# Splitting the ScalarE and VectorE parts of single steps into stages of their own in a Conformer/Mamba-2 trunk layer

## The chip, the cores and the metric

The kernel runs on one core of a Trainium2 chip. The metric is the device time of one execution in microseconds, the median of several runs. The core has a matrix engine (TensorE, PE in the profile), three engines for element-wise work (VectorE or DVE, ScalarE or ACT, GpSimd or POOL), and an engine that only issues transfers here (SyncE, SP). Each engine runs its own instructions strictly in the order in which the program issued them, and waits at an instruction until its operands are ready. The program writes these orders out by hand.

## The reference

One layer for two request groups (1024 prompt rows and 32 rows of a decoding group) with shared weights. All branch inputs come out of one wide projection:

```python
proj = x @ w_in + b_in
a_val, a_glu, a_gate, z, xbc, dt_raw, g_a, g_b, g_p = jnp.split(proj, idx, axis=-1)
u = a_val * jax.nn.sigmoid(a_glu)
u, new_buf_a = causal_dwconv(u, buf_a, conv_a_w, conv_a_b)            # width 31
u = jax.nn.silu(layer_norm(u, norm_a_g, norm_a_b)) * jax.nn.silu(a_gate)
out_a = u @ w_a_out
xbc, new_buf_b = causal_dwconv(xbc, buf_b, conv_b_w, conv_b_b)        # width 4
xs, Bm, Cm = jnp.split(jax.nn.silu(xbc), [...], axis=-1)
dt = jax.nn.softplus(dt_raw + dt_bias);  A = -jnp.exp(a_log)
y, h_new = ssd_scan(xs_h, dt, A, Bm, Cm, h0)                          # in chunks
y = y + d_skip * xs_h
out_b = gated_rmsnorm(y, z, gnorm_w) @ w_b_out                        # y * silu(z), rms over 4 groups
merged = sigmoid(g_a) * out_a + sigmoid(g_b) * out_b
ple = sigmoid(g_p) * (p @ w_ple)
x_new = layer_norm(alpha * x + merged @ w_out + ple, ln_g, ln_b)
```

The model width is 1024, the inner width of the Mamba-2 branch 2048 in 4 groups of 8 heads of 64, and the state has 128 columns. The outputs are the two groups' rows and the new caches and states. All is float32.

## The kernel before, in words

Tiles hold 128 channels in the partitions and the 1056 rows (NT) along the free dimension. A float32 product is made of three reduced-precision products: every operand is split into a high part (`act`, L198, on ScalarE) and a low part, the difference (`tt`, L184, on VectorE).

The program is a sequence of numbered slots. After a start (the per-layer embedding, the products for dt, the first splits) come 30 pair slots. Each computes two tiles of 128 channels of the wide projection with seven products j = 0 to 6 instead of eight (a Strassen scheme, with sums T3, T4 and so on of halves of x, and combined weights w_0 to w_6, whose high and low parts carry an h or l: w_5l is the low part for product 5). A product takes 24 matmuls. From `S_CL` = 31 on come 28 classic slots, each one tile of the projection in 72 matmuls. In most of the slots 31 to 67 an SSD chunk runs beside it: `load_l`, `decay`, then in the next slot `prep`, `pe_o`, `carry` and `pe_d`, and `update` at the start of the slot after that. From `S_OB` = 59 on come the slots of the output projection of the B branch, from `S_OA` = 71 those of the A branch, from `S_Q3` = 79 the last quarter of B, and `S_WO` = 83 begins the last product with w_out and the final LayerNorm.

What else is to be done is put beside these products by `at(slot, stage, fn)`. A slot runs its stages in a fixed order, and that order is the order on every engine. In a pair slot `ld0`, `ld`, `st`, `d0`, `a0` and `d1` come after the evacuation of product 0, `a1` after product 2, `pm` and `a2` after product 4, `d2` after product 5, `pe` and `end` at the close; the split of the next weights stands after every product. In a classic slot it is `ld0`, the weights' load, `ld`, `st`, `d0`, the weights' split, `a0`, `d1`, then the products' three column groups with `a1` after the first and `pm` and `a2` after the second, then `d2`, `pe`, `end`. The evacuations of TensorE's results are ScalarE instructions between the stages, so whatever stands ahead of them on ScalarE delays them.

The queue `fill` holds the taps of the A branch's convolution of width 31, 31 items a channel tile. `run_fill(limit)` issues them until the planner's sum of VectorE's modelled time in this slot, `dve[0]`, passes the limit: 2820 ns a product in a pair slot (less 300), 11000 in a classic slot, 14200 if the slot has a chunk. `ca_flush` in slot 34 issues what is left. Tiles of working memory come from pools; `tget` takes the one that has been free the longest, and waits (by its release) for a store that still reads it.

SP's queue carries the loads, and the stores as long as the slot is below 31; later stores go through GpSimd's queue. The combined weights come by accumulating transfers on GpSimd's queue in the pair phase.

The names that matter: `dt0` to `dt10` make dt and its decays (a softplus by series, a scan, two reciprocals, repacking), `DT9` is the slot of its transposes. `t_split` and `x_sum` make the operands of the products. `cw_load` and `cw_sum` read w_out for its column means. `z_tile` handles a tile of z with `gate`, `square`, `add`, `spill`. `ln_center`, `ln_square`, `ca_away` and `ln_var` make the channel LayerNorm's centred tiles and variance, with `A0` = 37. `y_load`, `y_hi` and `y_lo` bring back, scale and split the gated SSD result. `base_tiles` adds embedding and residual; `wo_load` and `wo_split` bring four tiles of w_out early.

Of the kernel before, what the change touches and what calls it, by code (L numbers as in the profile page):

```python
# [61 lines left out]
def pair_tiles():  # L62
# [6 lines left out]
    return [G(0), G(2), C(0), G(8), G(4), G(10), C(1), G(6), G(12), C(2), Z(14), G(14), C(3), Z(12), G(16), C(4), G(18),  # L69
# [67 lines left out]
def emit(nc, tc, I, O, ctx):  # L137
# [114 lines left out]
    busy = set()  # L252
# [54 lines left out]
    def slot(s, nm, nk, rhs, evac):  # L307
# [312 lines left out]
    def dt1():  # L620
# [5 lines left out]
        act(small[:H, 41:42], col(C_DT + 2, 1, H), AF.Sigmoid)
        act(small[:H, 42:43], col(C_DT + 2, 1, H), AF.Sigmoid, scale=-1.0)
        nc.vector.reciprocal(small[:H, 42:43], small[:H, 42:43])
        tt(small[:H, 41:42], small[:H, 41:42], small[:H, 42:43], ALU.mult)
# [22 lines left out]
    def dt3():
# [12 lines left out]
    def dt4():  # L665

        v, t, e = dtt["v"], dtt["t"], dtt["cum"]
# [4 lines left out]
    def dt5():
# [297 lines left out]
    def ssd_group(g, s0, XS, Bt_, Ct_):  # L970
# [15 lines left out]
        for i in range(9):  # L986
# [150 lines left out]
    def z_tile(g, j, zt, s):  # L1137
# [724 lines left out]
```

## Time and profile before

| | us |
|---|---|
| median of 3 runs | 1599.21 |
| lowest and highest | 1598.11, 1600.18 |
| the profiled execution | 1598.68 |
| its span | 1597.0 |
| TensorE busy | 1515.9 (95%) |
| VectorE busy | 1207.4 (76%) |
| ScalarE busy | 863.7 (54%) |
| mean granted TensorE clock | 0.979 |

The span is the time from the first to the last recorded instruction. Busy times overlap between engines. A granted clock of 1 is full speed; the profile gives it for every stretch, and a stretch in which TensorE had half its clock shows as a mean below 1. The row of a wait names the waiting engine's instruction and the instruction or transfer that released it, with the total, the count and the longest in us. Slot 1 begins at 44.41, slot 7 at 191.49, slot 30 at 664.69, slot 59 at 1144.37 and slot 79 at 1431.98.

### The profile page before, as it was taken

The page shows a single profiled execution, that of the slowest core. Times are in us where ns is not written, and L with a number is a line of the kernel's source. Part 1 is how long each engine was busy: PE and PEld are TensorE (multiplying, and loading weights), DVE is VectorE, ACT ScalarE, POOL GpSimd, SP SyncE. Part 2 cuts the span into 40 slices and gives each one's busy share as a digit, 9 for nine tenths or more (in the row PEclk, how much of TensorE's full clock was granted, in tenths as well). Part 3 has the DMA queues.
Part 4 walks back from the last instruction along what each step waited for, and adds up shares of the span by engine and source line. Part 5 has one row for each costly group of instructions (what it writes and reads, how often), then busy time and mean ns, then how long its engine had stood idle before and what let it go on. Part 6 is the DMA issues. An engine that isn't in the chain of part 4 may idle for free.

```text
span 1597.0 us, 27638 instructions
## 1 busy us (share of the span) xinstructions
PE 1515.9 (95%) x10967; PEld 1462.7 (92%) x10967; DVE 1207.4 (76%) x1647; ACT 863.7 (54%) x1491; POOL 288.1 (18%) x443
## 2 busy tenths in 40 slices
PE   7889999999999999998999889999998999999897
PEld 7889999999999999997999879889987989998897
DVE  6657898998988898789883768476856787577654
ACT  6536444444434443554774767678776366443333
POOL 1223343343333333211110110010000000000000
PEclk9989999999999999999999989999999999999998
DMA  9867978888676788447884574645473556545122
GB/s 313 239 173 177 268 199 228 238 205 210 161 180 167 180 220 206 108 134 240 268 261 146 159 181 110 182 116 140 163 234 93 158 178 234 199 177 183 31 90 74
DMA packets 156418, 288.43 MB, mean 181 GB/s; under 512 B 27120, under 2 KB 83456, under 8 KB 156288
## 3 DMA queue, kind: packets, MB, share of 16 engines
q1 hardware_dynamic: 112224, 176.60, 35.2%
q0 software_dynamic: 44064, 110.07, 27.7%
q8 instruction: 86, 1.41, 0.4%
q14 instruction: 44, 0.36, 0.1%
HBM read 226.14 MB, written 60.46 MB: 179 GB/s over the span
## 4 chain that ended last, share of the span: by engine, by line
PE 71%; DVE 10%; ACT 7%; DMA 6%; issue 5%; SPq 0%; POOL 0%; ACTq 0%; DVEq 0%; POOLq 0%
PE ps L211 70%; DVE acc_t L184 1%; ACT L_t L198 1%; DMA zt_u<-d_z 1%; DMA cat_u<-d_ca 1%; DVE cao_u L188 1%; DMA d_gate<-ga_t 1%; DMA yraw_t<-d_yn 1%; DMA zt_z<-d_z 1%; ACT whi L198 1%; PE ps L1017 1%; ACT L198 1%; DMA wq<-in_wp 1%; DVE cae_u L188 1%; SPq L201 0%
## 5 line engine op out<-in xcount | busy, mean ns | idle before, releaser
L493 POOL DMA_DIRECT2D s<-in_w x150 | 131.8, 907 | 260.3 <-DMA s<-in_w 204.4
L188 DVE SCALAR_TENSOR_TENSOR cae_u<-uin_u,par,cae_u 128x1086 f32<-128x1086 f32 x120 | 161.2, 1344 | 0.0
L188 DVE SCALAR_TENSOR_TENSOR cao_u<-uin_u,par,cao_u 128x1086 f32<-128x1086 f32 x112 | 150.5, 1344 | 0.0
L184 DVE TENSOR_TENSOR wlo<-wraw,whi 128x1024 fp32r<-128x1024 f32 x53 | 64.9, 1224 | 78.8 <-ACT whi L198 78.6
L198 ACT ACT_TABLE_LOAD x74 | 94.9, 1283 | 3.0 <-DMA zt_t<-d_z 0.9
L211 PE MATMUL ps<-t3l,w_4h 128*128 128x264 f32 x240 | 69.7, 291 | 6.9 <-ACT ga_t L198 6.9
L211 PE MATMUL ps<-n2l,w_2h 128*128 128x264 f32 x240 | 69.3, 289 | 7.0 <-ACT ga_t L198 7.0
L198 ACT ACTIVATE whi<-wraw 128x1024 fp32r<-128x1024 f32 x53 | 56.0, 1056 | 35.3 <-PE ps L211 26.2
L198 ACT ACTIVATE gb_t<-ps,par 128x528 f32<-128x528 f32 x32 | 22.5, 702 | 94.5 <-PE ps L211 90.5
L488 POOL DMA_DIRECT2D s<-in_w x84 | 46.3, 552 | 132.7 <-issue 40.0
L211 PE MATMUL ps<-t3h,w_4l 128*128 128x264 f32 x240 | 69.8, 291 | 0.0
L211 PE MATMUL ps<-t3h,w_4h 128*128 128x264 f32 x240 | 69.4, 289 | 0.0
L211 PE MATMUL ps<-n2h,w_2h 128*128 128x264 f32 x240 | 69.3, 289 | 0.0
L488 POOL DMA_DIRECT2D r<-in_w x85 | 61.1, 761 | 43.3 <-DVE w_0l L184 15.1
L211 PE MATMUL ps<-n2h,w_2l 128*128 128x264 f32 x240 | 68.9, 287 | 0.0
L211 PE MATMUL ps<-t4h,w_6h 128*128 128x264 f32 x240 | 68.4, 285 | 0.0
L211 PE MATMUL ps<-t4l,w_6h 128*128 128x264 f32 x240 | 68.1, 284 | 0.0
L211 PE MATMUL ps<-t4h,w_6l 128*128 128x264 f32 x240 | 67.9, 283 | 0.0
L198 ACT ACTIVATE ga_t<-ps,par 128x528 f32<-128x528 f32 x36 | 25.2, 700 | 57.4 <-PE ps L211 57.4
L211 PEld LDWEIGHTS ps<-t3l,w_4h 128*128 128x128 f32 x240 | 46.2, 192 | 7.2 <-ACT ga_t L198 7.2
L211 PEld LDWEIGHTS ps<-n2l,w_2h 128*128 128x128 f32 x240 | 46.1, 192 | 7.2 <-ACT ga_t L198 7.2
L198 ACT ACTIVATE ps<-ps 128x528 f32<-128x528 f32 x28 | 16.7, 595 | 64.2 <-PE ps L211 64.2
(1120 smaller groups left out, 6075.8 us busy)
## 6 DMA issues: line engine op xcount, KB each, us to landing
s<-in_w POOLq DMA_DIRECT2D x234, 256.0 KB, 4.7
r<-in_w POOLq DMA_DIRECT2D x85, 256.0 KB, 5.4
wraw<-in_w SPq DMA_DIRECT2D x27, 512.0 KB, 8.6
wraw<-in_wb SPq DMA_DIRECT2D x16, 512.0 KB, 3.9
E<-d_expa SPq DMA_DIRECT2D x56, 128.0 KB, 8.7
d_gate<-ga_t SPq DMA_DIRECT2D x12, 528.0 KB, 6.1
yraw_t<-d_yn SPq DMA_DIRECT2D x12, 528.0 KB, 6.4
L_z<-d_accp SPq DMA_DIRECT2D x12, 512.0 KB, 9.0
```

The costliest lines, as they stand in the source:

```text
L184: nc.vector.tensor_tensor(out, a, b, op)
L188: nc.vector.scalar_tensor_tensor(out, a, s, b, op0, op1)
L198: nc.scalar.activation(out, a, f, **kw)
L211: nc.tensor.matmul(out, l, r, start=start, stop=stop, skip_group_check=more)
L488: (nc.gpsimd if cur[0] else nc.sync).dma_start(t, pw_src(i, PARTS[n][0]))
L493: nc.gpsimd.dma_start(pr[i, n], pw_src(i, (PARTS[n] + ("12",))[k]), accum_op=ALU.add)
L1017: nc.tensor.transpose(pX[:nt, j * P:(j + 1) * P], XS[j][:, sl], ident)
```

## The change

Steps that had their ScalarE and VectorE parts in one stage get a stage for each. No matmul is added or removed. In detail:

- The T3 splits, T4 sums and T4 splits are issued in stages a0, d1 and a1 of slot 1, no longer ahead of it.
- The dt chain is cut into 18 steps instead of 13, spread over slots 2 to 9. `pk` goes; the repacked values live in `e`, and the reciprocal of 528 columns becomes two of 264.
- The loads and sums of w_out for the means (`cw_load`, `cw_sum`) go from slots 1 and 2 to slots 2, 3, 4, 7 and 8.
- The order of the gate pairs in the pair slots changes.
- `run_fill`'s limit in a classic slot counts 1100 for a chunk's slot and 2400 for the slot after it, on 11000.
- `z_tile`: gate from pm to d2, square from a2 to the next slot's a0, add from d1 to a1, spill from st to a1.
- The A branch's LayerNorm: centring from pm to d2, square from a2 to the next slot's a0, the store from st to a1, the variance from d1 to d2. The chain of u for t = 0 and 1 starts two slots later.
- y: scaling and high split in two stages; only k = 0, 1, 3 and 4 load in the slot of the scaling.
- `wo_load` and `wo_split` for m = 2, 3: loads from slots 79 and 80 to 73 and 74, splits from 80 and 81 to 74 and 75.
- `base_tiles`: one tile a stage (a1, d2) in place of both at once.

```diff
-    return [G(0), G(2), C(0), G(8), G(4), G(10), C(1), G(6), G(12), C(2), Z(14), G(14), C(3), Z(12), G(16), C(4), G(18),
+    return [G(0), G(2), C(0), G(4), G(6), G(16), C(1), G(8), G(10), C(2), G(12), Z(14), C(3), G(14), Z(12), C(4), G(18),
...
-    DT9 = 6
+    DT9 = 8
...
-        run_fill(14200.0 if ("pe", s) in busy else 11000.0)
+        run_fill(11000.0 + sum(busy[s]))
...
-            busy.add(("pe", s0 + i))
+            busy[s0 + i].append(1100.0)
+            busy[s0 + i + 1].append(2400.0)
...
     def dt7b():
-        pk = dtt["pk"]
-        a, b = pk[:, :2 * NQ], pk[:, 2 * NQ:]
-        tsc(b, a, -1.0, 1.0, ALU.mult, ALU.add)
-        dve[0] += 4500
-        nc.vector.reciprocal(b, b)
-        tt(a, a, b, ALU.mult)
-        tt(pk[:, NQ:2 * NQ], pk[:, NQ:2 * NQ], dtt["e"][:, :NQ], ALU.mult)
-        drop("e")
+        e = dtt["e"]
+        b = e[:, 3 * NQ:]
+        for j in (1, 2):
+            a = e[:, j * NQ:(j + 1) * NQ]
+            tsc(b, a, -1.0, 1.0, ALU.mult, ALU.add)
+            dve[0] += 2300
+            nc.vector.reciprocal(b, b)
+            tt(a, a, b, ALU.mult)
+        tt(a, a, e[:, :NQ], ALU.mult)
...
-    for sl_, stage, fn in ((2, "d0", dt1), (3, "d0", dt2), (3, "a1", dt3), (3, "a2", dt4), (4, "d0", dt5), (4, "d1", dt6), (4, "a1", dt7),
-                           (4, "d2", dt7b), (5, "a0", dt8), (5, "end", dt8b), (6, "end", dt8c), (DT9, "pe", dt9), (7, "a0", dt10)):
+    for sl_, stage, fn in ((2, "d0", dt1), (2, "a0", dt1e), (2, "a2", dt1b), (2, "d2", dt1f), (3, "d1", dt2), (3, "pm", dt2b),
+                           (4, "a1", dt3), (4, "pm", dt4), (5, "d0", dt5), (5, "a0", dt5b), (5, "pm", dt6), (6, "a1", dt7),
+                           (6, "pm", dt7b), (7, "a1", dt8), (7, "end", dt8b), (8, "end", dt8c), (DT9, "pe", dt9),
+                           (DT9 + 1, "a0", dt10)):
...
-    for q in range(2):
-        t_split("t3", (0, 1), q)
-    x_put((0, 1))
...
-    for q in range(2):
-        x_sum("T4", q)
-        t_split("t4", (1, 0), q)
+    at(1, "a0", t3_split)
+    at(1, "d1", t4_sum)
+    at(1, "a1", t4_split)
...
-        at(s, "pm", gate)
-        at(s, "a2", square)
-        at(s + 1, "d1", add)
+        at(s, "d2", gate)
+        at(s + 1, "a0", square)
+        at(s + 1, "a1", add)
...
-        at(s + 1, "st", spill)
+        at(s + 1, "a1", spill)
...
+    CW = (2, 2, 3, 3, 4, 7, 8, 8)
     for i, m in enumerate((2, 3, 0, 1, 4, 5, 6, 7)):
-        at(1 + i // 4, "ld", cw_load, i)
-        at(1 + i // 4, "d2", cw_sum, i)
+        at(CW[i], "ld", cw_load, i)
+        at(CW[i], "d2", cw_sum, i)
...
-        late = k < 5 or 8 <= k < 12
+        late = k in (0, 1, 3, 4)
         at(s if late else s - 1, "ld", y_load, k)
-        last = k == 3 or 8 <= k < 12
-        at(s, "a2" if last else "a1" if late else "a0", y_hi, k)
-        at(s, "d2" if last else "a2" if late else "a1", y_lo, k)
+        at(s, "a1" if late else "d1", y_scale, k)
+        at(s, "a2" if late else "a1", y_hi, k)
+        at(s, "d2" if late else "pm", y_lo, k)
...
-        at(c, "pm", ln_center, t)
-        at(c, "a2", ln_square, t)
-        at(c + 1, "st", ca_away, t)
-        todo[(c + 1, "d1")].insert(0, (ln_var, (t,)))
-
-        c = B + (3, 4, 8, 9, 9, 10, 10, 11)[t]
+        at(c, "d2", ln_center, t)
+        at(c + 1, "a0", ln_square, t)
+        at(c + 1, "a1", ca_away, t)
+        at(c + 1, "d2", ln_var, t)
+
+        c = B + (5, 6, 8, 9, 9, 10, 10, 11)[t]
...
     for m in (2, 3):
-        at(S_WO - 6 + m, "ld", wo_load, m)
-        at(S_WO - 5 + m, "a1", wo_split, m)
+        at(S_OA + m, "ld", wo_load, m)
+        at(S_OA + m + 1, "a1", wo_split, m)
...
         at(s + 1, "a0", sig)
-        at(s + 1, "a1", mul)
-        at(s + 2, "ld", fetch, lambda m: I["xT"][m * P:(m + 1) * P, :])
-        at(s + 2, "d1", add)
-        at(s + 3, "st", spill)
+        for j, b in enumerate(("a1", "d2")):
+            at(s + 1, b, mul, j)
+            at(s + 2, b, add, j)
+        for j, a in enumerate(("ld", "a1")):
+            m = ns[j]
+            at(s + 1, a, fetch, d_ple[m])
+            at(s + 2, a, fetch, I["xT"][m * P:(m + 1) * P, :])
+            at(s + 3, "st", lambda m=m, t=ts[j]: store(d_base[m], t, t))
```

More of the change, by code (lines that the diff above doesn't have):

```diff
@@ L251, in emit @@
     todo = defaultdict(list)
-    busy = set()
+    busy = defaultdict(list)
     fill = deque()
@@ L624, in dt1 @@
         tt(small[:H, 40:41], col(C_DT, 1, H), col(C_DT + 1, 1, H), ALU.add)
[L626 to L629, printed above, removed]
         for q in range(4):
@@ L632, in dt1, with dt1e, dt1f, dt1b @@
                 t1[:H, q * NQ:(q + 1) * NQ], ALU.add, ALU.add)
+    def dt1e():
+        act(small[:H, 41:42], col(C_DT + 2, 1, H), AF.Sigmoid)
+        act(small[:H, 42:43], col(C_DT + 2, 1, H), AF.Sigmoid, scale=-1.0)
+    def dt1f():
+        nc.vector.reciprocal(small[:H, 42:43], small[:H, 42:43])
+        tt(small[:H, 41:42], small[:H, 41:42], small[:H, 42:43], ALU.mult)
+    def dt1b():
+        v, t, e = dtt["v"], dtt["t"], dtt["e"]
         act(t[:, :NQ], v[:, :NQ], AF.Abs)
@@ L648, in dt2 @@
         stt(e, q, 2.0, dtt["v"][:, :NQ], ALU.mult, ALU.add)
+        drop("v", "t")
     h = slice(0, H)
@@ L665, in dt4 @@
     def dt4():
[L667 removed]
+        v, t, e = dtt["p96"], dtt["z2"], dtt["cum"]
         tsc(v[h], dtt["t1"][h], small[h, 41:42], -1.0, ALU.mult, ALU.mult)
@@ L670, in dt4 @@
         nc.vector.tensor_tensor_scan(e[h], t[h], v[h], 0.0, ALU.mult, ALU.add)
+        drop("t1")
     def dt5():
@@ L676, in dt5, with dt5b @@
         tt(blk(z2, 1), blk(e, 1), tot(0), ALU.add)
+    def dt5b():
+        p96, z2, e = dtt["p96"], dtt["z2"], dtt["cum"]
         act(blk(p96, 1), blk(e, 1))
@@ L680, in dt5 @@
         act(z2[h, TP:NT], e[h, TP:NT])
-        drop("v", "t1", "cum")
     def dt6():
-        p96, z2, t = dtt["p96"], dtt["z2"], dtt["t"]
+        p96, t = dtt["p96"], dtt["cum"]
         c3 = lambda x: x[h, :TP].rearrange("p (c l) -> p c l", c=8)
@@ L809, in emit, with t3_split, t4_split, t4_sum @@
     pw_add(1, "s3", 1)
-    for q in range(2):
-        x_sum("T4", q)
-        t_split("t4", (1, 0), q)
-    x_put((1, 1))
-    x_put((1, 0))
-    new_psum("ps1")
+    new_psum("ps1")
+    def t3_split():
+        for q in range(2):
+            t_split("t3", (0, 1), q)
+        x_put((0, 1))
+    def t4_split():
+        for q in range(2):
+            t_split("t4", (1, 0), q)
+        x_put((1, 0))
+    def t4_sum():
+        for q in range(2):
+            x_sum("T4", q)
+        x_put((1, 1))
+    at(1, "a0", t3_split)
+    at(1, "d1", t4_sum)
+    at(1, "a1", t4_split)
     def plain(t):
@@ L1276, in y_load, with y_scale @@
         load(yraw[k], d_yn[k])
-    def y_hi(k):
+    def y_scale(k):
         rb = yrb[k // 4]
@@ L1282, in y_hi @@
             tput(rb)
+    def y_hi(k):
         yq[k // 4].append((tget((P, NT), F32R, f"y{k}h"), tget((P, NT), F32R, f"y{k}l")))
@@ L1497, in fetch @@
         def fetch(src):
-            for m in ns:
-                t = tget(name="bt")
-                load(t, src(m))
-                tmp.append(t)
+            t = tget(name="bt")
+            load(t, src)
+            tmp.append(t)
         def sig():
@@ L1505, in sig, with mul, add @@
                 act(t, t, AF.Sigmoid)
[L1507 to L1529 removed]
+        def mul(j):
+            p_ = tmp.pop()
+            tt(ts[j], ts[j], p_, ALU.mult)
+            tput(p_)
+        def add(j):
+            x = tmp.pop()
+            stt(ts[j], x, ALPHA, ts[j], ALU.mult, ALU.add)
+            tput(x)
+            cb_sum(ns[j], ts[j])
+        at(s + 1, "a0", sig)
+        for j, b in enumerate(("a1", "d2")):
[6 more added lines that the diff above has]
+            at(s + 3, "st", lambda m=m, t=ts[j]: store(d_base[m], t, t))
     def half_load(q):
```

36 lines of the change are left out of this document (11 added, 25 removed).

## The prediction

> **What bounds the kernel now.** I read the page's busy times and chain first, then TensorE's waits, then busy times slot by slot, and last the timeline at the longest waits.
>
> The page of the kernel before:
>
> ```profile
> span 1597.0 us, 27638 instructions
> PE 1515.9 (95%) x10967; PEld 1462.7 (92%) x10967; DVE 1207.4 (76%) x1647; ACT 863.7 (54%) x1491; POOL 288.1 (18%) x443
> PE 71%; DVE 10%; ACT 7%; DMA 6%; issue 5%; SPq 0%; POOL 0%; ACTq 0%; DVEq 0%; POOLq 0%
> L188 DVE SCALAR_TENSOR_TENSOR cae_u<-uin_u,par,cae_u 128x1086 f32<-128x1086 f32 x120 | 161.2, 1344 | 0.0
> ```
>
> TensorE is busy for 95% of the span, and the chain runs on it for 71%. The change touches no matmul, so it can win only the places where TensorE stands still or runs at half clock. The L188 row is a convolution tap; 1.34 us each matters below. TensorE's waits (total, times, longest), from the same kernel:
>
> ```profile
> PE ps L211 <- ACT ga_t L198: 13.9, 2, 7.0
> PE ps L211 <- DVE ps L184: 9.3, 5, 7.0
> PE ps L211 <- ACT acc_t L198: 7.0, 3, 5.0
> PE ps L211 <- DVE w_5l L184: 5.7, 3, 3.1
> PE ps L211 <- ACT hT_u L198: 4.1, 1, 4.1
> ```
>
> The large ones are few and single. I take them in order of time.
>
> **The change part by part.** Slots are measured against undisturbed ones. The windows (start and end, length, busy time and count of PE, PEld, DVE, ACT and POOL, granted clock, DMA share, GB/s) of slots 1 to 3 together, slot 5, slot 14 (undisturbed) and slot 47 (undisturbed, classic):
>
> ```profile
> 44.41:126.17 81.76, 66.95 (x506) 66.11 (x505) 51.63 (x81) 33.88 (x60) 24.22 (x36) 0.90 0.73 200
> 147.05:170.23 23.18, 20.86 (x170) 20.64 (x169) 21.10 (x24) 12.82 (x25) 8.22 (x12) 1.00 0.73 179
> 335.52:356.09 20.57, 20.57 (x170) 20.57 (x169) 19.78 (x22) 8.64 (x14) 7.47 (x11) 1.00 0.87 234
> 956.43:971.77 15.34, 15.34 (x109) 14.43 (x107) 12.48 (x16) 12.47 (x23) 1.61 (x3) 1.00 0.37 96
> ```
>
> *A, slots 1 to 3.* The excess is 81.76 − 3 × 20.57 = 20.05 us. The timeline names its causes (start, duration, instruction, idle before it and what released it):
>
> ```profile
> 55.68 1.08 ACT L198 ACTIVATE t4h<-xraw_t 128x1056 fp32r<-128x1056 f32 x1 [2.49 <-DVE xraw_t L188]
> 57.40 0.59 PE L211 MATMUL ps<-n2l,w_2h 128*128 128x264 f32 x1 [6.99 <-ACT ga_t L198]
> ...
> 87.25 1.98 DVE L188 SCALAR_TENSOR_TENSOR dt_t<-dt_u,small,dt_u 32x264 f32<-32x264 f32 x4 [7.73 <-DMA d_gate<-ga_t]
> 89.31 0.42 ACT L198 ACTIVATE dt_t<-dt_t 128x264 f32<-128x264 f32 x1 [10.15 <-DVE dt_t L188]
> 92.68 0.59 PE L211 MATMUL ps<-t3l,w_4h 128*128 128x264 f32 x1 [6.94 <-ACT ga_t L198]
> ```
>
> In slot 1 ScalarE's evacuation of product 1 stands behind the t4h splits, which wait for VectorE's T4 sums. In slot 2 it stands behind dt1's Abs, which waits for VectorE, whose tile waits for a store that lands at 87.23. The change puts the T3 splits, T4 sums and T4 splits behind the evacuation of product 0. Product 0 is evacuated by about 47.6, the splits (two pairs of 1.08 and about 1.3 us, the two engines overlapping) run to 51.9, the sums to 54.4, the T4 splits to 58.3, and w_5l ends near 59.0; product 5 starts at 44.41 + 5 × 2.94 = 59.1. So it just fits, with about 0.5 us left over. In slot 2 VectorE still waits for the landing, but ScalarE's Abs (dt1b) comes only after product 4, so the evacuations pass. Slot 3's chain is split likewise. The eight cw loads, all queued on SP in slots 1 and 2, move partly to slots 2, 3, 4, 7 and 8; the DMA share of 0.73 leaves room. **−19.5.** Bounds: −20 if all goes, −10 if the splits or the weights arrive one product late in each slot.
>
> *B, slots 4 to 9.* The dt chain's DVE work moves on: the scan to slot 4, the halves of the reciprocal to slot 6. dt7b becomes seven VectorE instructions instead of four over the same columns; the three more, of 264 columns, I put at 0.42 each by the Abs of that width above, and at nothing on the path, since slot 14 runs without a stall with VectorE at 19.78 of 20.57. POOL's two memsets go with dt3 from slot 3 to slot 4, onto a tile that is free, so the weight adds queued behind them don't wait. But what VectorE does next is chosen by the planner, which issues taps until the modelled VectorE time of the slot reaches 2.82 us per product. The queue is empty until late in slots 4 and 8, when the channel tile of the pair before is queued; by then the dt chain and the base adds have used less of the budget than before, so the rest goes at once: by a count through the code 7 items at the end of slot 4 (before: 3) and 8 at the end of slot 8 (before: 5). Seven items at 1.26 to 1.34 us keep VectorE until 10 us into slot 5. About 9.2 us of its own work stand ahead of w_5l (two taps 2.6, four weight splits 2.8, dt5's two and the sums 3.8), so w_5l would end at +19.4 where product 5 needs it at +14.85: a stall of 4.6. Slot 9 the same way: VectorE is free at +8.4, w_5l at +17.75, a stall of 2.95. What a late w_5l does shows in slot 5 of before, and a short stall in slot 34 against what a half clock costs:
>
> ```profile
> 163.66 0.68 DVE L184 TENSOR_TENSOR w_5l<-s,w_5h 128x512 fp32r<-128x512 f32 x1
> 164.39 0.39 PE L211 MATMUL ps<-x4h_t,w_5l 128*128 128x264 f32 x1 [2.32 <-DVE w_5l L184]
> ...
> 740.82 0.55 PE L211 MATMUL ps<-cb_t,hT_z 128*128 128x128 f32 x1 [2.55 <-DVE cb_y L188]
> ```
>
> The first cost slot 5 2.6 us and no clock (1.00 in its window), the second was followed by half clock (0.92 in slot 34's window, in C). Its price comes from slots 34 and 52, both with 114 matmuls: 17.77 − 16.51 = 1.26 (windows in C and E). I take 1.7 for the 4.6 stall, since a wait that long costs more than one half window, and 1.2 for the 2.95 one. With 0.4 in slot 7, that is 4.6 + 1.7 + 2.95 + 1.2 + 0.4 = 10.8 against 2.6 that go: **+8.2.** Bounds: −2.6 (the bursts are absorbed) to +11.
>
> *C, slots 33 to 35.* The reordered pairs leave 7 items at the flush in slot 34 where 2 were left, and slot 33's limit now counts 1100 plus 2400 on 11000 (14500, not 14200), slot 32's 12100.
>
> ```profile
> 713.74:734.16 20.42, 16.14 (x100) 14.44 (x99) 20.37 (x20) 11.79 (x21) 2.67 (x5) 0.92 0.88 293
> 734.16:754.48 20.32, 17.77 (x114) 15.79 (x113) 20.18 (x26) 8.85 (x19) 3.24 (x6) 0.92 0.66 224
> 754.48:769.84 15.36, 15.36 (x108) 14.45 (x107) 11.99 (x16) 13.07 (x25) 2.76 (x6) 1.00 0.87 240
> ```
>
> VectorE is full in 33 and 34 (20.37 of 20.42) and not in 35. One tap fewer ahead of slot 33's chunk gains 1.3. Five more in slot 34, 5 × 1.34 = 6.7 us, delay the state update at the start of slot 35 beyond the 3.4 us of idle that VectorE has there (15.36 − 11.99): 3.3, and 1.2 for the clock. **+3.2.** Bounds: −4 (slot 35's slack, 15.36 − 11.99, takes them) to +6.5.
>
> *D, slots 43 to 46.* Four slots take 79.33 us where 4 × 15.34 = 61.4 would do: 17.9.
>
> ```profile
> 877.10:956.43 79.33, 67.94 (x430) 62.29 (x428) 56.52 (x83) 57.92 (x104) 10.23 (x19) 0.89 0.65 174
> ...
> 876.75 1.09 ACT L198 ACTIVATE zt_u<-cb_t 128x1056 f32<-128x1056 f32 x1 [5.53 <-DVE cb_t L184]
> 885.29 0.58 PE L211 MATMUL ps<-cb_z,hT_u 128*128 128x128 f32 x1 [4.06 <-ACT hT_u L198]
> ...
> 933.00 1.26 DVE L184 TENSOR_TENSOR cat_u<-cat_u,lnS_y 128x1056 f32<-128x1056 f32 x1 [7.21 <-DMA cat_u<-d_ca]
> 935.53 0.69 PE L211 MATMUL ps<-L_z,X 128*64 128x128 f32 x4 [6.95 <-DVE ps L184]
> ```
>
> In 43 ScalarE waits in its square for a late z tile, and the chunk's decay, prep and hT stand behind it; in 45 VectorE waits in ln_center for a late cat tile, and the carry that TensorE needs stands behind it. Now the gate and the centring come in d2, after those, and the square in the next slot's a0. The transfers are not earlier. So the wait stays on the engine but what is queued behind it is now the taps, the pe stage and the next slot's update: in 44 I expect 1.6 (a wait of the statistics), in 46 a stall of 4.4 with 1.2 of clock, because the cat tile of slot 45 lands 17 us after that slot's start (932.98) whatever the order. 17.9 becomes 7.2: **−10.7.** Bounds: −17.9 to −3.
>
> *E, slots 52 and 53.* The same wait in small, and *F, slots 59 to 68*:
>
> ```profile
> 1032.07:1050.03 17.96, 16.51 (x114) 14.52 (x113) 9.75 (x15) 14.15 (x24) 2.67 (x5) 1.00 0.41 146
> 1050.03:1067.54 17.51, 16.32 (x114) 14.54 (x113) 13.28 (x23) 14.63 (x28) 2.11 (x4) 1.00 0.34 79
> 1144.37:1314.96 170.59, 157.85 (x1043) 143.47 (x1041) 119.75 (x188) 103.67 (x183) 4.81 (x9) 0.98 0.57 180
> ...
> 1205.27 0.66 PE L211 MATMUL ps<-y0l_t,whi 128*128 128x352 f32 x1 [5.01 <-ACT acc_t L198]
> ```
>
> Against TensorE's busy time in each, E loses 1.4 + 1.2, and the same move of square and gate takes it away: **−2.6.** F's ten slots take 170.59 where 153.4 would do: 17.2 too much. Slot 62's 5.01 is an evacuation behind VectorE's adds of z tiles; with the adds in a1 and the u chain two slots later, I leave 3.5 of the 9.2 in slot 62, and give back 2.5 at slot 65, where u1 and y8, y9 make 18 us of VectorE work in one slot. The rest (y_scale split from y_hi, loads a slot earlier) gains about 3.4. **−6.6.** Bounds for E and F together: −20 to 0.
>
> *G, slots 80 to 82.* Two splits of w_out weights, one ScalarE and one VectorE instruction each, move from slots 80 and 81 to 74 and 75, with their loads on SP.
>
> ```profile
> 1453.76 1.04 ACT L198 ACTIVATE woh_t<-wor_t 128x1024 fp32r<-128x1024 f32 x1
> 1454.84 1.23 DVE L184 TENSOR_TENSOR wol_t<-wor_t,woh_t 128x1024 fp32r<-128x1024 f32 x1 [0.42 <-ACT woh_t L198]
> ```
>
> There 0.42 of idle and 1.23 of work, 1.65 together, put every following evacuation back: twice 1.65 goes, **−3.3**. In slots 74 and 75 they lie beside the out-projection's matmuls; if VectorE were full there, they would cost the same 1.65 each, so nothing is gained. Bounds: −6 to 0. The base tiles' split into single adds and loads on SP at a1 I cost at nothing: VectorE's work is the same, and SP's later entries in those slots are weights for two slots on.
>
> Sum: −19.5 + 8.2 + 3.2 − 10.7 − 2.6 − 6.6 − 3.3 = −31.3. The profiled execution took 1598.68 (span 1597.0 and 1.7 around it): 1567.4. The median shown is 0.5 above it: **1567.9 us.**
>
> **The rivals.** R1, slower: every gate and centring now in d2 pushes the state update past the time at which the chunk's off-diagonal products need it, some 4 us after a slot's start, in each of the 37 slots with a chunk. It eats the 31.3 from 0.85 us a slot on; at 1.1 it gives 1567.9 + 40.7 = 1609. Against it: slot 47 has 12.48 us of VectorE work in 15.34, so 2.9 us of slack.
>
> R2, the bursts don't bite: VectorE catches up before w_5l and the update are due. B is then −2.6 and C −1.3, together 15.3 less: 1553; with half of that, 1560. For it: w_5l needs VectorE only in order, and slot 35 has 3.4 us of idle. Against it: 740.82 and 164.39 above are such bursts in the kernel before.
>
> R3, the waits only move: transfers that land late in slots 43, 45, 52 and 62 stop the update or the next evacuation instead. D, E and F then give −6 together instead of −19.9: 1582. For it: the idle times of 7.21 and 5.53 are released by a DMA or by its first user, and few loads are moved.
>
> R4, the early slots are paced by the weights: A gives −10: 1577. For it the DMA share of 0.73 to 0.87; against it, no wait of TensorE on a weight load is among the rows.
>
> R5, the clock doesn't drop after the shorter stalls in slots 9, 35 and 46. By the rows this is open: the wait of 2.32 lost none, that of 2.55 did; the 2.95, 3.3 and 4.4 forecast are longer than both, so I keep the loss. Three times 1.2 less: 1564.3. The Trainium skill ("TensorE: Matmul & The Clock Gate", section "What's actually happening") has the throttle come back after an idle window of about 3.4 us that runs free; by it gaps of 2.95 and 3.3 us would mostly keep the clock. The trace has half clock after a gap of 2.55 and none after 2.32, so the stated window does not decide it here.
>
> R6: the stages do no more than rename the waits everywhere, and the time stays within 0.2% (3 us), about what a measurement of this kernel can tell from no change.
>
> **How the numbers follow.** My forecast 0.36, R5 0.08, R2 0.18, R3 0.22, R4 0.08, R1 0.05, R6 0.03. All but R1 and R6 are faster: 0.92, same 0.03, slower 0.05. The range leaves out R1, R6 and the far ends of R2 and R3: 1553 to 1590. The likeliest case's own range is 1559 to 1577.
>
> **What would show it.** Slots 1 and 2 at 20.6 to 21.5 and clock 1.00 (A); the waits on ga_t gone. A w_5l wait in slots 5 and 9 with taps ahead of it (B). A wait on the carry or hT in slot 35 (C) and slot 46 (D), and none in 43. Slot 62 under 20 (F). No split between the evacuations of slots 80 to 82 (G). I am wrong if slots 5, 9 and 35 run at 20.57 and 15.35 (too slow a forecast), or if loads released in 43 to 62 keep the same waits under other names.

## The result and the profile after

The changed kernel takes 1579.98 us (median; 1578.33 to 1580.76) against 1598.66 us for the kernel before (the median of four runs; it was 1599.21 of the three above). The ratio is 0.9887, with a 95% interval of 0.9864 to 0.9909. The gain is 18.7 us where 31.3 were forecast; the time lies inside the range of 1553 to 1590. The profiled execution took 1579.97 with a span of 1578.1, so the two profiles differ by 18.9 us of span.

The page's busy times and chain by engine, and TensorE's longest waits, of the changed kernel:

```profile
PE 1513.6 (96%) x10967; PEld 1464.6 (93%) x10967; DVE 1205.3 (76%) x1650; ACT 865.5 (55%) x1492; POOL 289.7 (18%) x443
PE 68%; DVE 8%; DMA 6%; ACT 5%; issue 3%; SPq 0%; POOL 0%; DVEq 0%; ACTq 0%; POOLq 0%
...
PE ps L211 <- DVE w_5l L184: 12.9, 4, 5.0
PE ps L211 <- DVE cb_y L188: 5.9, 2, 3.4
PE ps L211 <- ACT gb_t L198: 3.7, 1, 3.7
PE ps L211 <- DVE acc_t L184: 3.6, 1, 3.6
PE ps L211 <- DVE acc_z L184: 3.2, 1, 3.2
```

The busy times have hardly moved. The waits have: the two on ga_t (13.9 us), the carry's (9.3) and hT_u's (4.1) are gone or small, and w_5l's have grown from 5.7 to 12.9. The windows of the changed kernel, in the order slots 1 to 3, 4 to 9, 33 to 35, 43 to 46, 52 and 53, 59 to 68, 79 to 81 (columns as in the prediction):

```profile
45.26:113.26 68.00, 64.31 (x506) 64.10 (x505) 41.66 (x68) 31.24 (x55) 24.84 (x35) 0.95 0.82 212
113.26:253.65 140.39, 129.16 (x1020) 127.89 (x1018) 114.03 (x136) 63.45 (x115) 48.29 (x69) 0.95 0.70 179
713.28:773.99 60.71, 52.04 (x317) 47.12 (x315) 59.80 (x70) 33.85 (x63) 8.95 (x17) 0.89 0.79 262
880.97:946.89 65.92, 62.75 (x430) 57.69 (x428) 55.37 (x81) 52.47 (x93) 9.96 (x19) 1.00 0.72 205
1022.44:1056.77 34.33, 32.53 (x225) 29.04 (x224) 23.14 (x38) 26.45 (x50) 5.90 (x11) 1.00 0.40 126
1133.47:1300.19 166.72, 157.69 (x1044) 145.51 (x1042) 120.03 (x189) 104.84 (x184) 4.82 (x9) 0.97 0.56 185
1418.98:1453.70 34.72, 34.72 (x219) 34.72 (x217) 25.19 (x47) 15.79 (x23) 0.00 (x0) 1.00 0.34 122
```

Against the kernel before, stretch by stretch (us; the forecast of G was for slots 80 to 82):

| stretch | before | after | difference | forecast |
|---|---|---|---|---|
| A, slots 1 to 3 | 81.76 | 68.00 | −13.8 | −19.5 |
| B, slots 4 to 9 | 127.05 | 140.39 | +13.3 | +8.2 |
| C, slots 33 to 35 | 56.10 | 60.71 | +4.6 | +3.2 |
| D, slots 43 to 46 | 79.33 | 65.92 | −13.4 | −10.7 |
| E, slots 52 and 53 | 35.47 | 34.33 | −1.1 | −2.6 |
| F, slots 59 to 68 | 170.59 | 166.72 | −3.9 | −6.6 |
| G, slots 80 to the end | 153.40 | 147.55 | −5.9 | −3.3 |
| slot 73 | 12.72 | 14.17 | +1.5 | 0 |
| everything else | | | −0.2 | 0 |

"Everything else" is small only in sum: the time ahead of slot 1 grew by 0.9 and slot 30 by 1.4, and slots 10 to 29 took 2.3 less, of which the last section tells.

The instructions at which it decides, from the timeline of the changed kernel, for slots 1, 4 and 5, 9, 35, 44 and 65:

```profile
65.38 0.63 ACT L198 ACTIVATE w_2h<-s 128x512 fp32r<-128x512 f32 x1 [7.46 <-DMA s<-in_w]
66.65 0.59 PE L211 MATMUL ps<-t4l,w_6h 128*128 128x264 f32 x1 [3.69 <-ACT gb_t L198]
...
126.86 0.69 DVE L184 TENSOR_TENSOR w_5l<-s,w_5h 128x512 fp32r<-128x512 f32 x1 [6.26 <-ACT w_5h L198]
153.22 0.59 PE L211 MATMUL ps<-x4h_t,w_5l 128*128 128x264 f32 x1 [4.60 <-DVE w_5l L184]
...
245.93 0.59 PE L211 MATMUL ps<-x4h_t,w_5l 128*128 128x264 f32 x1 [4.97 <-DVE w_5l L184]
...
759.95 1.41 PE L211 MATMUL ps<-cb_t,hT_z 128*128 128x128 f32 x5 [3.36 <-DVE cb_y L188]
...
908.35 0.79 PE L211 MATMUL ps<-zt_u,ones 128*32 128x352 f32 x6 [1.21 <-DVE zt_u L184]
...
1237.86 0.66 PE L211 MATMUL ps<-y4l_t,whi 128*128 128x352 f32 x1 [3.62 <-DVE acc_t L184]
```

Slot 1 has a new wait: an evacuation (gb_t) stands on ScalarE behind the split of w_2, and that waited 7.46 us for its weights. Slots 5 and 9 have the late w_5l that was forecast, 35 the late state update, and in 65 an accumulation on VectorE is late.

### The profile page after: what moved, and what is told of

Its sections match the earlier page's. It is cut to its first block, busy times and chain, and to the rows that moved or that the text cites. A ratio compares the mean times of both kernels' runs of the same rounds, so it can differ in the third digit from the quotient of the medians.

```text
span 1578.1 us, 27638 instructions
## 1 busy us (share of the span) xinstructions
PE 1513.6 (96%) x10967; PEld 1464.6 (93%) x10967; DVE 1205.3 (76%) x1650; ACT 865.5 (55%) x1492; POOL 289.7 (18%) x443
## 4 chain that ended last, share of the span: by engine, by line
PE 68%; DVE 8%; DMA 6%; ACT 5%; issue 3%; SPq 0%; POOL 0%; DVEq 0%; ACTq 0%; POOLq 0%
PE ps L211 67%; DVE cae_u L188 1%; DMA s<-in_w 1%; DMA cat_t<-d_ca 1%; ACT L_t L198 1%; DMA zt_u<-d_z 1%; DVE cao_u L188 1%; DMA cat_z<-d_ca 1%; ACT whi L198 1%; DMA yraw_t<-d_yn 1%; DMA cw_z<-in_wo 1%; PE ps L1045 1%; DMA L_z<-d_accp 1%; ACT L198 0%; DVE yraw_t L188 0%
## 5 line engine op out<-in xcount | busy, mean ns | idle before, releaser
L488 POOL DMA_DIRECT2D r<-in_w x85 | 65.9, 834 | 22.9 <-DVE w_0l L184 17.9
L211 PE MATMUL ps<-t3l,w_4h 128*128 128x264 f32 x240 | 68.5, 285 | 0.0
L211 PEld LDWEIGHTS ps<-t4l,w_6h 128*128 128x128 f32 x240 | 46.6, 194 | 4.4 <-ACT gb_t L198 3.9
L211 PEld LDWEIGHTS ps<-t4h,w_6l 128*128 128x128 f32 x240 | 46.6, 194 | 0.0
```

The lines of the kernel that those rows point to most:

```text
L211: nc.tensor.matmul(out, l, r, start=start, stop=stop, skip_group_check=more)
L488: (nc.gpsimd if cur[0] else nc.sync).dma_start(t, pw_src(i, PARTS[n][0]))
```

## The experiments

Each was compared with the kernel before on its own chip; the times below are medians, and the slots come from each run's profile. "The changed kernel" has 1579.98.

**Slot 1: whose transfers.**

```diff
-    CW = (2, 2, 3, 3, 4, 7, 8, 8)
+    CW = (4, 4, 5, 5, 6, 7, 8, 8)
```

> The changed kernel with one edit: the w_out loads for the means in slots 4, 4, 5, 5, 6, 7, 8, 8, none in 2 and 3. Theory (shared transfers): in slot 1 the last accumulating transfer of w_2's weights, issued at 57.87 and landed at 65.29, runs beside two of these loads, issued at 57.30 and 58.47; without them it lands by about 63, the 3.7 us wait in slot 1 falls under 1.7 and slot 1 goes from 26.8 to 21 to 24.5; the moved sums cost up to 2 us in slots 4 to 6; in all 1 to 5 us faster than the changed kernel. Rival (chain): the transfers for one weight follow one another and take 5 to 7 us each whatever else runs; slot 1 stays at 26 to 27.

Measured: 1572.12, ratio 0.9843 (0.9826 to 0.9859). Slot 1 takes 21.3 us instead of 26.8. ScalarE's split of w_2 begins at 60.23, 17.0 after the slot's start, where it began 20.1 after it. The windows of slot 1 and of slots 1 to 3, and the split:

```profile
43.24:64.53 21.29, 20.73 (x171) 20.52 (x169) 17.80 (x23) 13.27 (x21) 7.39 (x10) 1.00 0.77 193
43.24:105.44 62.20, 61.64 (x506) 61.42 (x505) 38.62 (x64) 31.52 (x55) 24.79 (x35) 1.00 0.85 224
...
60.23 0.63 ACT L198 ACTIVATE w_2h<-s 128x512 fp32r<-128x512 f32 x1 [4.27 <-DMA s<-in_w]
```

So two 512 KB loads beside the last accumulating transfer were worth 5.5 us in slot 1: that transfer took 3.74 us from issue to landing, and 7.42 in the changed kernel. Slot 9 fell too (27.7 to 20.8) and slot 5 did not (27.9): with the sums of w_out now in slots 4 to 6 the planner leaves more taps for slot 8, so that 5 run there and 11 in slot 9, where it was 1 and 15.

**Slots 1 and 2: which part of the change freed them.** The T3 and T4 stages of slot 1 (t3_split, t4_sum and t4_split as in the change) put into the kernel before, with

```diff
-        at(1 + i // 4, "ld", cw_load, i)
-        at(1 + i // 4, "d2", cw_sum, i)
+        at((1, 1, 1, 2, 2, 2, 2, 3)[i], "ld", cw_load, i)
+        at((1, 1, 1, 2, 2, 2, 2, 3)[i], "d2", cw_sum, i)
```

> The kernel before with only the T3 and T4 stages of the change in slot 1 (and the w_out loads for the means in slots 1, 1, 1, 2, 2, 2, 2, 3, as the tiles don't suffice otherwise). Theory: the 7.0 us wait of product 2 for ga_t in slot 1 goes, and what is late next is the weights of the following slot (w_2, by accumulating transfers beside the w_out loads), so slot 1 goes from 29.4 to 26 to 28 and not to 20.6; slot 2 keeps its 30 us, since its wait is the dt chain's; 1 to 4 us faster than the kernel before (about 1595). Rival: nothing else was late; slot 1 falls to 20.5 to 22 and the gain is 7 to 9 us.

Measured: 1588.76, ratio 0.9947 (0.9926 to 0.9968), 8 us less than before. But slot by slot both sides of the expectation missed: slot 1 did not get shorter and slot 2 lost its whole stall, with the dt chain as before.

```profile
42.98:72.39 29.41, 23.33 (x170) 22.91 (x169) 20.12 (x25) 13.21 (x21) 9.74 (x13) 0.88 0.97 279
72.39:92.94 20.55, 20.55 (x170) 20.55 (x169) 11.36 (x21) 10.06 (x19) 7.71 (x11) 1.00 0.78 192
...
65.80 0.63 ACT L198 ACTIVATE w_2h<-s 128x512 fp32r<-128x512 f32 x1 [8.58 <-DMA s<-in_w]
```

In slot 1 the split of w_2 waits 8.58 us for its weights, as in the changed kernel, with a DMA share of 0.97. To see what freed slot 2, two runs moved only the w_out loads in the kernel before. The first has the diff above and nothing else:

> The kernel before with the w_out loads for the means in slots 1, 1, 1, 2, 2, 2, 2, 3 and nothing else: the run with the T3 and T4 stages had this too, and its slot 2 fell from 30.4 to 20.55 while its slot 1 stayed at 29.4. Theory (loads ahead of the store): slot 2's wait was the gate store's, which stood behind w_out loads on SP's queue until 76.77 and shared the transfers until 87.23; with one load fewer in slot 1 it goes out early, and slot 2 falls to 20.5 to 22 here as well, slot 1 stays at 28.5 to 30. Rival (stages): the T3 and T4 stages made slot 2 short by another order of tiles; slot 2 stays at 28 to 31 and the time within 3 us of the kernel before.

Measured: 1595.58, ratio 0.9993 (0.9981 to 1.0004), no difference. Slot 2 takes 28.0 us: my theory fell. The second has the slots 1, 1, 2, 2, 3, 3, 4, 4:

> The kernel before with the w_out loads for the means in slots 1, 1, 2, 2, 3, 3, 4, 4 and nothing else. Theory (loads ahead of the store): two loads ahead of the gate store in slot 2; slot 2 falls to 20.5 to 23 although the dt chain is as before; slot 1 keeps its 7 us wait for the T4 splits, 28 to 30, since that is an order on ScalarE; slots 3 and 4 grow by under 2; 6 to 10 us faster than the kernel before. Rival (dt chain): ScalarE's Abs behind VectorE holds the evacuations however early the store lands; slot 2 stays at 27 or more.

Measured: 1587.12, ratio 0.9931 (0.9912 to 0.9949). Slot 2 takes 26.9 us, on the edge of the rival's case, slot 3 20.45 in place of 21.99. SP's queue in the run with the loads spread and in the run with the T3 and T4 stages, and VectorE's first dt instruction, which waits for the store's landing:

```profile
71.06 1.46 SPq L201 DMA_DIRECT2D cw_t<-in_wo  x2
73.00 0.33 SPq L205 DMA_DIRECT2D d_gate<-ga_t  x1
83.25 1.98 DVE L188 SCALAR_TENSOR_TENSOR dt_t<-dt_u,small,dt_u 32x264 f32<-32x264 f32 x4 [4.05 <-DMA d_gate<-ga_t]
...
56.57 0.90 SPq L201 DMA_DIRECT2D cw_u<-in_wo  x2
72.93 0.33 SPq L205 DMA_DIRECT2D d_gate<-ga_t  x1
78.64 1.98 DVE L188 SCALAR_TENSOR_TENSOR dt_t<-dt_u,small,dt_u 32x264 f32<-32x264 f32 x4 [0.54 <-DMA d_gate<-ga_t]
```

The first three rows are of the former, the others of the latter. The store goes out at the same time, 73.0 and 72.9. With two w_out loads just ahead of it, VectorE goes on 10.2 us later; with the loads already out by 57.5, 5.7 us later. The kernel before had four loads ahead of it and 10.5 us (76.77 to 87.25), the changed kernel none and 5.0 (68.59 to 73.58). So slot 2's stall hangs on what is in flight beside the store; whether the loads hold it in SP's queue or on the transfer engines, these runs do not tell. With a landing after 5.7 us the old dt chain, Abs ahead of the evacuations and all, runs without a stall.

**Slot 5: the time of the taps, or their number.** First the taps joined the queue earlier in the slot:

```diff
-        at(s, "d2", later)
+        at(s, "a1", later)
```

> The changed kernel with one edit: a channel tile's taps join the queue in stage a1 (after product 2) in place of d2, so that the planner can spread its budget over four products and not spend it after product 6. Theory (burst): slots 5 and 9 go from 27.5 and 27.7 to 20.5 to 21.5, no other slot gets longer, 12 to 14 us faster than the changed kernel (about 1567). Rival (volume): VectorE has more work in slots 4 to 9 than time, and the stall of w_5l comes up in slots 4, 6 or 8 in its place; the sum of slots 4 to 9 stays above 136 of 140.4 us.

Measured: 1580.19, ratio 0.9883 (0.9851 to 0.9915): nothing gained. Slots 4 to 9 together, slot 4 alone, and the first tap of the tile:

```profile
112.06:252.77 140.71, 129.28 (x1020) 127.38 (x1018) 115.39 (x137) 63.23 (x115) 48.55 (x70) 0.96 0.72 180
112.06:133.43 21.37, 21.01 (x171) 20.59 (x169) 11.17 (x15) 12.36 (x20) 6.00 (x10) 1.00 0.63 155
...
128.06 0.78 DVE L193 TENSOR_SCALAR cao_u<-uin_u,par 128x1086 f32<-128x1086 f32 x1
```

The sum is 140.7 against 140.4, the rival's case. The taps did begin earlier, 16.0 us after the start of slot 4 in place of 22.3. But they could not begin before w_5l, whose high part ScalarE splits late, behind an evacuation and dt3's copies: VectorE stood there for 6.26 us in the changed kernel (at 126.86) and 7.45 here, and was busy for only 11.17 us of slot 4. Then fewer taps in slot 4:

```diff
-            run_fill(2820.0 * (j + 1) - 300.0)
+            run_fill((2820.0 if s > 9 else 2820.0) * (j + 1) - 300.0 - {4: 6000.0}.get(s, 0.0))
```

> The changed kernel with one edit: the planner's limit in slot 4 is 6000 lower, so 3 items go there and not 7 (the other four go later, and 12 are left for the flush, not 7). The run with the taps queued earlier left slots 4 to 9 as long as before the edit (140.7 against 140.4): spreading the burst is not enough. Theory (volume): VectorE stands idle for 6.3 us in slot 4 behind ScalarE's split of w_5, the planner counts that time as free, and the 7 items it issues are more than VectorE can make up; with four fewer slot 5's wait of 4.6 goes to under 0.5 and slot 5 to 20.5 to 21.5, slot 9 gets shorter too as the queue isn't empty in slot 8; slot 35 grows to 25 to 28 by five more items in the flush; in all 3 to 10 us faster than the changed kernel. Rival (dt chain): the dt steps, not the taps, hold w_5l; slot 5 stays above 25.

Measured: 1573.79, ratio 0.9862 (0.9829 to 0.9895). The windows of slots 4 to 9, slot 5 and slot 35:

```profile
114.39:241.18 126.79, 124.60 (x1020) 123.75 (x1018) 107.20 (x130) 63.35 (x115) 47.00 (x68) 1.00 0.75 196
134.85:155.31 20.46, 20.46 (x170) 20.46 (x169) 20.43 (x25) 8.89 (x17) 8.27 (x13) 1.00 0.75 198
739.41:768.31 28.90, 17.89 (x108) 16.70 (x107) 28.27 (x34) 13.06 (x25) 4.10 (x8) 0.76 0.64 210
```

Four items fewer free slots 5 and 9 wholly (140.4 to 126.8 for the six), with the dt chain in place. VectorE is full in slot 5, 20.43 of 20.46: the number was the matter. Slot 35 pays 7.4 us, 28.9 instead of 21.5; 25 to 28 was expected.

**Slots 34 and 35: the flush.** Half of it one slot later (`ca_flush` takes half of the queue in slot 34 and the rest in 35):

```diff
-    at(S_CL + 3, "d2", ca_flush)
+    at(S_CL + 3, "d2", ca_flush, 2)
+    at(S_CL + 4, "d2", ca_flush)
```

> The changed kernel with one edit: the flush of the tap queue is halved, four items at the end of slot 34 and three at the end of slot 35. Theory (flush): the 7 items in slot 34 hold the state update of slot 35; slot 35 goes from 21.5 to 15.4 to 17, slot 36 from 15.3 to at most 16.5; 4 to 6 us faster than the changed kernel (about 1575). Rival (moved): three taps at the end of slot 35 hold slot 36's update just the same; slot 36 at 18 or more and a gain under 2 us.

Measured: 1575.82, ratio 0.9857 (0.9836 to 0.9877). Slot 35 falls to 15.3, slot 36 rises to 17.7, slots 33 to 36 together go from 76.0 to 73.1, where other executions with the code of the changed kernel there took 75.0 to 75.6: a part is moved, a part is gained. Then a budget by which nothing is left to flush:

```diff
-            run_fill(2820.0 * (j + 1) - 300.0)
+            run_fill((2900.0 if s > 9 else 2820.0) * (j + 1) - 300.0 - {}.get(s, 0.0))
```

> The changed kernel with one edit: the planner's budget is 2900 a product from slot 10 on, not 2820, so that no item is left at the flush in slot 34. Theory: the stalls in slots 34 and 35 are the taps' (6 in slot 33, 7 in the flush); slot 35 goes to 15.3 to 15.5, slot 34 to 17 at most, slots 10 to 29 stay at 20.46; 8 to 11 us faster than the changed kernel. Rival: VectorE has no room for half a tap more a slot; slots 10 to 29 get 0.2 us or more longer each (4 us or more) and the gain is under 5.

Measured: 1573.47, ratio 0.9849 (0.9827 to 0.987). Slots 33 to 35, and 10 to 29, where those of the changed kernel take 60.7 and 409.2:

```profile
717.73:766.41 48.68, 46.07 (x317) 42.45 (x315) 43.84 (x55) 33.83 (x63) 8.95 (x17) 1.00 0.90 300
...
252.35:668.46 416.11, 412.82 (x3362) 411.77 (x3361) 383.32 (x433) 178.49 (x301) 150.37 (x214) 1.00 0.78 203
```

The stalls of 34 and 35 are the taps': 12 us go there. Both sides of the expectation hold in part, since slots 10 to 29 give back 416.1 − 409.2 = 6.9, of which 2.3 is the slower steady rate told of at the end.

**Slots 43 and 45: whose gain.**

```diff
-        at(s, "d2", gate)
-        at(s + 1, "a0", square)
-        at(s + 1, "a1", add)
+        at(s, "pm", gate)
+        at(s, "a2", square)
+        at(s + 1, "d1", add)
...
-        at(s + 1, "a1", spill)
+        at(s + 1, "st", spill)
```

> The changed kernel with z_tile's four steps back in the stages of before (gate pm, square a2, add d1, spill st), the LayerNorm's steps left as changed. Theory (order of the queue): the gains of slots 43, 52, 53 and 62 are this edit's; slot 43 goes from 15.3 back to 20 to 22, 62 from 17.5 to 22 to 25, 52 and 53 by up to 1.5, slot 44 from 19.5 down to 16.7 to 18, and slot 45 stays at 15.3 because that is the LayerNorm's; 8 to 14 us slower than the changed kernel. Rival: the LayerNorm's move freed 43 as well; the time stays within 4 us of the changed kernel.

Measured: 1584.43, ratio 0.9925 (0.9901 to 0.995), 4.5 slower than the changed kernel. Slots 43, 44 to 46, and 61:

```profile
875.46:897.60 22.14, 18.25 (x109) 17.03 (x107) 15.19 (x20) 16.42 (x34) 4.05 (x8) 0.85 0.87 264
897.60:949.22 51.62, 48.73 (x325) 44.85 (x323) 40.96 (x64) 41.16 (x73) 6.27 (x12) 0.97 0.59 161
1164.99:1186.03 21.04, 17.14 (x109) 15.64 (x107) 12.26 (x16) 16.74 (x30) 1.08 (x3) 0.92 0.51 155
```

Slot 43's stall is back, to 22.1 us, while slot 45 stays at 15.3: 43 is the z stages' gain and 45 the LayerNorm's. Slot 62 went to 18.1 only, from 17.5; the wait of its kind came up in 61 (21.0 instead of 15.9). Slots 52 and 53 moved by 0.6 together, the other way. Slots 44 and 73 got shorter by 2.8 and 1.4, without the waits of the late statistics. Slots 43, 44, 52, 53, 61, 62 and 73 add up to 7.8 more, near the 8 expected; the total is below it because the rest, with the same code, took 3.3 less in this profile than in the changed kernel's (slot 46 3.8 more, the other places 7.1 less). Two executions of the same code differ that much in places, so a difference of a few us between two profiles shows an effect only in the slots that the edit touches.

**Slots 65 and 66: order or volume.**

```diff
-        at(s, "a1" if late else "d1", y_scale, k)
+        at(s, "a1" if late or 8 <= k < 12 else "d1", y_scale, k)
```

> The changed kernel with one edit: y_scale for k = 8 to 11 in stage a1 (after the first evacuation) in place of d1. Theory (order): the two scalings of 1.3 us each stand on VectorE ahead of the first group's accumulations, so TensorE waits 3.6 and 3.2 us for a bank in slots 65 and 66 and loses clock after it; slots 65 and 66 go from 22.5 and 20.4 to 15.3 to 16.5 each, the kernel 9 to 11 us faster than the changed kernel (about 1570). Rival (volume): u1 with y8 and y9 is too much VectorE work for slot 65 whatever the order; slot 65 stays above 19 and the gain is under 4 us.

Measured: 1575.6, ratio 0.9863 (0.9844 to 0.9882). Slots 65 and 66, and the wait left in 65:

```profile
1223.71:1246.16 22.45, 17.27 (x108) 15.40 (x107) 17.30 (x25) 13.87 (x21) 0.00 (x0) 0.92 0.39 111
1246.16:1262.26 16.10, 15.38 (x109) 14.39 (x107) 13.56 (x21) 7.95 (x16) 0.00 (x0) 1.00 0.15 41
...
1241.89 0.48 PE L211 MATMUL ps<-L_t,X 128*64 128x128 f32 x2 [4.03 <-DVE ps L184]
```

In 66 the order was all of it. In 65 the wait only moved from the accumulation to the carry (4.03), which stands behind u1's product. So u was taken out of that slot as well:

```diff
-        c = B + (5, 6, 8, 9, 9, 10, 10, 11)[t]
+        c = B + (4, 5, 8, 9, 9, 10, 10, 11)[t]
```

> The changed kernel with two edits: y_scale for k = 8 to 11 in a1 (as in the first run, which mended slot 66 and not 65), and u for t = 0 and 1 in slots 63 and 64, one earlier, where no y tile is split. Theory (collision): in slot 65 the carry stands behind u1's product, which waits for ScalarE's splits of y8 and y9; without u1 slot 65 goes from 22.5 to 15.3 to 16.5 and 66 to 15.3 to 16.5, 63 and 64 stay under 16; 9 to 12 us faster than the changed kernel. Rival: the u chain holds up whatever slot it is in, and 63 or 64 goes to 18 or more.

Measured: 1572.92, ratio 0.9851 (0.9826 to 0.9876). Slots 63 to 66 take 67.3 us in place of 73.5: 65 falls to 16.9, 66 to 15.7, and 63 and 64 rise by 1.8 and 2.2. Against the run before it, 65 and 66 lost 6.0 us and 63 and 64 gained 4.0: two thirds of that wait went with the u chain, and one third was the slot's. The rival has the larger share.

**Together.** The later y_scale, u one slot earlier, the w_out loads in slots 4 to 8, a limit 3000 lower in slot 4, and a budget of 2900 from slot 15 on:

> The changed kernel with what the runs before found, together: y_scale for k = 8 to 11 in a1, u for t = 0 and 1 in slots 63 and 64, the w_out loads in slots 4, 4, 5, 5, 6, 7, 8, 8, the planner's limit in slot 4 lower by 3000 (4 items, not 7) and its budget 2900 a product from slot 15 on (2 items left for the flush, not 7). Theory: each mends its own place (slot 1 -5.5, slots 5 and 9 -7 to -13, slots 34 and 35 -4 to -8, slots 63 to 66 -6): 22 to 32 us faster than the changed kernel, 1549 to 1558. Rival: VectorE's work is only pushed from slot to slot, and at most half of it stays: 1565 or more.

Measured: 1562.7, ratio 0.978 (0.976 to 0.9801): 17 us below the changed kernel, the best of all, and 5 short of the expected interval. Slots 1 to 3 take 62.5, 33 to 36 68.5 (from 76.0), 63 to 66 67.2. Slots 4 to 9 keep 131.1, of which slot 7 has 25.1 (in the changed kernel 22.8); slots 44 and 46 take 20.4 and 20.3 (from 19.5 and 15.8). So the work was pushed on in part, and the rival has its share. About 3 of the 5 us short are the slower steady rate of the pair slots in the profiled execution (20.57 and not 20.46), told of at the end.

## Why the prediction was right, and where its sizes were off

All seven signs came as forecast. The sizes missed by 1.4 to 5.7 us, and the time fell into the range in part by luck: the gains in D and G came out 5.3 larger than forecast and hid as much of the misses in A, B, C, E and F.

*A, −19.5, measured −13.8.* The two waits on ga_t went. The step that failed is the transfers': "the DMA share of 0.73 leaves room" hid two things. In slot 1 the weights of w_2 were late next, which moving the loads showed to be 5.5 us of shared transfers; R4 was a part of the truth. In slot 2 I put the gain down to ScalarE's Abs coming after product 4. The run with the T3 and T4 stages shows that the old order has no stall once the store lands in 5.7 us; in the changed kernel it took 5.0. The reordering of dt1 is therefore not shown to be needed.

*B, +8.2, measured +13.3.* Slot 5's wait is 4.60, as worked out, slot 9's 4.97 in place of 2.95, and slot 7 takes 22.84 in place of 21.0. Each of the first two cost 2.2 to 2.4 more in half clock (27.46 − 20.46 − 4.60 = 2.4), where the sum had 1.7 and 1.2: the half clock lasted 6.83 us each time, of which 2.04 and 2.58 were still the wait, and the rest, at half clock, costs half its length, 2.4 and 2.1. The wording of the cause failed: it is not that the budget goes at once at the end of the slot. Begun 6 us earlier, the taps cost the same. The planner counts as free the time in which VectorE stands behind ScalarE, and so issues more than fits.

*C, +3.2, measured +4.6.* The wait in slot 35 is 3.36 (worked out: 3.3). Slot 35's half clock cost 21.50 − 15.31 − 3.36 = 2.8, not 1.2 (again 6.83 us, 1.19 of them in the wait); the 1.3 gained in slot 33 came (1.55).

*D, −10.7, measured −13.4.* Slot 43 and 45 both at 15.3, and in 44 waits of 1.73 and 1.21 where 1.6 was put. The 4.4 in slot 46 did not come in this execution: the cat tile of slot 45 landed 13.3 us after that slot's start, and not 17. Where it landed later, the forecast stall was there, as in the combined kernel, at 16.2 us after the start (first row: the changed kernel; then the combined one):

```profile
929.04 1.26 DVE L184 TENSOR_TENSOR cat_z<-cat_z,lnS_y 128x1056 f32<-128x1056 f32 x1 [1.85 <-DMA cat_z<-d_ca]
...
914.81 1.26 DVE L184 TENSOR_TENSOR cat_z<-cat_z,lnS_y 128x1056 f32<-128x1056 f32 x1 [4.49 <-DMA cat_z<-d_ca]
921.21 0.35 PE L211 MATMUL ps<-cb_z,hT_u 128*128 128x128 f32 x1 [3.14 <-DVE cb_z L188]
```

Slot 46 took 15.8 us in the changed kernel, 20.3 in the combined one and 19.4 in the one with half the flush. So D's mechanism was right, and some 4 us of its gain were luck.

*E, −2.6, measured −1.1:* slot 53 kept a wait of 1.80, again of the statistics. The same kind of wait (1.62) is slot 73's +1.5, which the sum had at nothing. R3 was right in these small pieces, and in slot 46 in the runs just named.

*F, −6.6, measured −3.9.* Slot 62 fell by 7.1 (5.7 forecast), and 63, 64 and 67 by 5. Slots 65 and 66 rose by 11.2 where 2.5 was put: the collision in 65 was named, the y_scale of y10 and y11 ahead of the first accumulation in 66 was not.

*G, −3.3, measured −5.9.* 1.94 of it is slot 81's split. The other 1.65 of the sum was not there to win: slot 80 took 11.61 us before already, like slot 79. The rest lies behind slot 82's start, 124.41 us against 128.28. Other kernels with the changed code there took 122.8 to 126.3, and those with the code before 127.2 to 128.9, so a gain is there and its size is uncertain; what made it was not tested.

*The rivals.* R1 did not come: slots 47 to 51 take 75.55 us together, and took 75.64 before. R2 did not: the taps bit harder. R5 did not: the waits of 4.97 in slot 9 and 3.36 in slot 35 cost clock, and slot 46 had none. But the bound that the prediction drew between 2.32 and 2.55 is none: the length of a wait alone does not decide, as the last section shows. R6 did not: the time is 1.1% lower.

## What to carry to other kernels

A planner's modelled time of an engine is too low by what that engine stands behind another: look, in each slot where it issues filler work, for the idle time ahead of the engine's first late instruction, and take the filler out of that slot's budget before spreading it. When a step is split between engines to free a queue, ask for each queue what stands next behind the old culprit, including the transfers in flight beside the one that is waited for; here the next ones were the weights in slot 1 and the carry in slot 65.

## What the hardware showed that was not expected

The same 528 KB store landed in time for VectorE to go on 5.0 to 5.7 us after its issue with no w_out load just ahead of it, and 10.2 to 10.6 us with two to four of them, issued 0.5 to 2.9 us earlier.

Whether a wait costs clock is not set by its length. Slots 65 and 53 have waits of 3.62 and 1.80 us in the changed kernel, and waits of the same length in the run with fewer taps in slot 4. First the waits of that run, then the windows of its slots 65 and 53, then those of the changed kernel:

```profile
1235.81 0.43 PE L211 MATMUL ps<-y4l_t,whi 128*128 128x352 f32 x1 [3.62 <-DVE acc_t L184]
1044.72 0.50 PE L211 MATMUL ps<-zt_t,ones 128*32 128x352 f32 x3 [1.80 <-DVE zt_t L184]
...
1225.24:1246.01 20.77, 15.69 (x108) 14.42 (x107) 16.89 (x25) 12.28 (x20) 0.00 (x0) 1.00 0.39 116
1034.06:1053.71 19.65, 17.85 (x114) 16.07 (x113) 13.46 (x23) 14.65 (x28) 2.16 (x4) 0.91 0.29 71
...
1227.29:1249.75 22.46, 18.19 (x108) 16.92 (x107) 16.89 (x25) 12.28 (x20) 0.00 (x0) 0.85 0.36 108
1038.67:1056.77 18.10, 16.30 (x114) 14.52 (x113) 13.45 (x23) 14.66 (x28) 2.15 (x4) 1.00 0.32 77
```

In one execution the long wait kept the clock and the short one lost it; in the other it was the reverse. The clock records of the traces show why. Between slots 1 and 81 of all fourteen profiles, half clock comes in stretches of one to four steps of 3.413 us, and they begin on a grid of such steps that runs through the execution: in the changed kernel at 151.19, 243.35 and 1236.62, which lie 27 and 291 steps apart. Half clock followed wherever TensorE had waited for 1.92 us or more within one step, and nowhere after 1.78 or less (waits of 1.4 us and longer); in between, both occur. The wait of 3.62 that kept the clock is cut by the grid into 1.86 and 1.76, the one that lost it into 2.38 and 1.24; the 1.80 that lost it lies whole in one step, the other is cut into 1.36 and 0.45. So the clock terms of such a sum depend also on where in a step the wait falls, and that differs from one execution to the next.

The Trainium skill ("TensorE: Matmul & The Clock Gate", section "What's actually happening") has the throttle return after at least one idle window of about 3.4 us that runs free; the steps of 3.41 us here agree with its length, but a wait of 1.8 us within one of them was already enough.

Undisturbed pair slots take either 20.46 or 20.573 us throughout an execution, never between, both on the same chip, with a granted clock of 1.00 in either. The profile before shows 20.573 and the one after 20.46. Slots 10 to 29 differ by 2.3 us for that reason alone, which the table has under everything else. The change is not shown to be its cause: the kernel before with its loads spread ran at 20.46, and the combined kernel at 20.573. What sets the rate stays open.
